# Twelve instead of eight pairs of row tiles by seven products in the second feed-forward product, with weight sums formed by adding transfers

## The chip, the core and the metric

The kernel runs on one core of one Trainium2 chip. The metric is the device time in microseconds of one execution. The engines that matter are TensorE (PE: matmuls, with PEld for its weight loads), VectorE (DVE), ScalarE (ACT), GpSimd (POOL) and SyncE (SP); SP and POOL, and here and there ACT, issue the transfers (DMA) between the chip's memory (HBM) and the on-chip memory (SBUF). Matmul results stand in eight banks of PSUM, 128 partitions x 512 float32 each.

## The reference

One layer of an encoder: 512 tokens, model width 1024. After a mixing part (gated MLP and attention) comes the feed-forward part, whose second product is what changes:

```python
h = h + rms_norm(mix_out, norm_mix_post)
n2 = rms_norm(h, norm_mlp_pre)
hid = jnp.square(jax.nn.relu(n2 @ w_up))       # (512, 4096)
mlp_out = hid @ w_down                         # w_down: (4096, 1024)
h = h + rms_norm(mlp_out, norm_mlp_post)
```

All values are float32. The kernel multiplies in float32r: each operand is split into a high part (rounded) and a low part (the rest), and a product is three matmuls, high x high, high x low, low x high.

## The kernel before

**Stages.** The mixing part, then the first feed-forward product, whose result `hid` stands in SBUF as four tiles of eight row tiles (128 rows of the inner width 4096 each, by 512 tokens), three in the pool `hida` and the last in `hidb`; then the second product, in which `hid` is the stationary operand and `w_down` moves. Its result needs all eight banks: four token tiles of 128 x two column halves of 512. The program names them as quarters: X = tokens 0 to 255, columns 0 to 511; W = the same tokens, columns 512 to 1023; Y and Z the same columns for tokens 256 to 511. Each quarter is two banks.

**Plain row tiles.** `plain(f2)` (L1045) loads 1 MB, two row tiles of `w_down`, on SP (L1048), splits `hid` and the weights, and for each row tile adds into all eight banks: 8 x 3 = 24 matmuls (`acc3`, L1041 to L1043). 16 of the 32 row tiles are done so (`F7 = KF - 2 * N7`, `N7 = 8`).

**Seven products.** The other 16 row tiles form two blocks (`c`) of four pairs. In each block `hid` is cut into a11, a12 (tokens 0 to 255) and a21, a22 (tokens 256 to 511), `w_down` into b11, b12 and b21, b22 (the first index is the half of the pair, the second the column half). Seven products of sums replace eight: (a11 - a21) x (b22 - b12), a11 x b11, s2 x (b11 - b12 + b22) with s2 = a22 - a11 + a21, (a11 + s2) x (b22 - the last sum), (a12 - s2) x b22, a22 x (b21 - the sum), a12 x b21. One product of one block is 24 matmuls, which the code calls a chunk (half of it a piece).

**Sums before.** The sums of weights stand in `tsum` (pool `sumpool`) and in `t1`, and DVE forms them: `b22 - tsum` in `first_sums` (L1098), `tsum + b11` and `b21 - tsum` in `two` (L1091), `b22 - tsum` into `t1` (L1150). The activations' sums are formed in place in `hid` and in `s2` (L1099, L1101, L1124, L1125).

**Splits.** `split_into` (L79, L80) is an ACT copy (high) and a DVE subtraction (low). Weight splits go into the tag `hl` of the pool `wback` (five buffers), activation splits into `hhl` (`d0pool` for the first, then `dpool`, three buffers), raw weights into the tag `raw` (two buffers of 1 MB).

**The eight buffers n2.** The tag `n2` of `n2pool` has eight buffers of 512 KB. In this stage it holds, in program order: `gain`, two `b22` and `s2` for block 0, the same for block 1, `v`, four `t1`, and at the end `h2` and two result tiles `o2`.

**What sets the order.** The program lists work in program order; a planner then simulates it and writes each engine's order, and gives out the buffers. `tc.issue_after(ins)` keeps what stands in it behind `ins` on the engine of `ins`. Each engine and each DMA-issuing queue then works strictly in its written order, waiting on semaphores.

**Order of the quarters before.** Plain row tiles 0 to 9; Y += (a11 - a21) x tsum; X and Y by a11 x b11 and s2 x tsum in turn; `v` = Y + X's sum (L1133); plain row tiles 10 to 15; Z and W in turn; Y and X, the last block one token tile after the other. What a quarter had gathered before a product that others share is copied away (`r22`, `p1`, `r12`, `z0`, in a buffer of `hida`) and put back by DVE sums (L1130 to L1142, L1176 to L1178). `weigh` and `finish` (L1156 to L1172) then do the norm: ACT sums squares, DVE multiplies by `gain`, POOL takes the power (L96), DVE scales and adds `h2` (L1166), SP writes the halves out (L1168). `h2` is read back from memory by POOL (L1158).

Of the kernel before, what the change touches and what calls it, by code (L numbers as in the profile page):

```python
# [16 lines left out]
P = 128  # L17
# [19 lines left out]
def block_kernel(ctx: ExitStack, tc: tile.TileContext, x, norm_mix_pre, w_in, b_gate, ln_v_gain, ln_v_bias,  # L37
# [987 lines left out]
    N7 = 8  # L1025
    F7 = KF - 2 * N7
    FA = 10
# [17 lines left out]
    def plain(f2, order):  # L1045
# [4 lines left out]
        for j in range(2):  # L1050
            wh, wl = split_back(raw[:, j], [D])
            for t, hf in order:
                acc3(accs[t][hf], (hh[:, j, tsl[t]], hl[:, j, tsl[t]]), (wh[:, halves[hf]], wl[:, halves[hf]]),
                     f + j == 0, f + j in (FA - 1, F7 - 1))

    w7 = w_down[F7 * P:].rearrange("(c j h p) d -> c h p j d", p=P, h=2, j=4)

    def block(c, h, hf):
        raw = raw_down()
        raw = raw.rearrange("p a (b d) -> p (a b) d", d=512)  # L1060
        nc.sync.dma_start(raw, w7[c, h, :, :, halves[hf]])
        return raw

# [6 lines left out]
    def chunk(ps, h, w, stop):  # L1070
        for i in range(2):
            piece(ps, h, w, i, stop and i == 1)

    def piece(ps, h, w, i, stop=False):
        (hh, hl), (wh, wl) = h, w[i]
        for j in range(2):
            for t in range(2):
                acc3(ps[t], (hh[:, 2 * i + j, tsl[t]], hl[:, 2 * i + j, tsl[t]]), (wh[:, j], wl[:, j]), False, stop and j == 1)

    order = [(t, hf) for t in range(4) for hf in range(2)]  # L1080
    y_first = [(2, 0), (3, 0), (0, 0), (1, 0), (0, 1), (1, 1), (2, 1), (3, 1)]
    for f2 in range(3):
        plain(f2, order)
    blk = [hid[F7 // 8 + c].rearrange("p (j h) s -> p j h s", h=2) for c in range(2)]
    a11, a12, a21, a22 = [[b[:, :, h, z * 256:z * 256 + 256] for b in blk] for z in range(2) for h in range(2)]
    tsum = sumpool.tile([P, N7, 512], F32, name="tsum")
    tsum = [tsum[:, 4 * c:4 * c + 4] for c in range(2)]
    s2 = []

    def two(out, x, y, op):  # L1090
        nc.vector.tensor_tensor(out, x, y, op=op)  # L1091

    def first_sums(c):
        nc.sync.dma_start(tsum[c], w7[c, 0, :, :, halves[1]])
        for i in range(0, 4, 2):
            b22 = n2pool.tile([P, 2, 512], F32, name="b22", tag="n2")
            nc.sync.dma_start(b22, w7[c, 1, :, i:i + 2, halves[1]])
            nc.vector.tensor_tensor(tsum[c][:, i:i + 2], b22, tsum[c][:, i:i + 2], op=ALU.subtract)  # L1098
        nc.vector.tensor_tensor(a21[c], a11[c], a21[c], op=ALU.subtract)  # L1099
        s2.append(n2pool.tile([P, 4, 256], F32, name="s2", tag="n2"))  # L1100
        nc.vector.tensor_tensor(s2[c], a22[c], a21[c], op=ALU.subtract)  # L1101

    with tc.issue_after(joined.ins):
        first_sums(0)
    plain(3, order)
    with tc.issue_after(joined.ins):
        first_sums(1)
    plain(4, y_first)
    keep = hida.tile([P, 8, S], F32, name="hid")
    p1, r22, r12, z0 = [keep[:, 2 * i:2 * i + 2] for i in range(4)]  # L1110
    for dst, src in ((r22, Y), (p1, X)):
# [7 lines left out]
    for c in range(2):
        b11 = block(c, 0, 0)  # L1120
        h, w = h_split(a11[c]), w_split(b11)
        two(tsum[c], tsum[c], b11, ALU.add)
        h6, w6 = h_split(s2[c]), w_split(tsum[c])
        nc.vector.tensor_tensor(a11[c], a11[c], s2[c], op=ALU.add)  # L1124
        nc.vector.tensor_tensor(s2[c], a12[c], s2[c], op=ALU.subtract)  # L1125
        for i in range(2):
            piece(X, h, w, i, c == 1 and i == 1)
            piece(Y, h6, w6, i, c == 1 and i == 1)
# [6 lines left out]
    z_first = [(2, 1), (3, 1), (0, 1), (1, 1), (0, 0), (1, 0), (2, 0), (3, 0)]  # L1135
    for f2 in range(FA // 2, F7 // 2):
        plain(f2, z_first)
    for i in range(2):
        nc.scalar.activation(z0[:, i], Z[i], AF.Copy)
    nc.vector.tensor_tensor(r22, v, r22, op=ALU.subtract)  # L1140
    nc.vector.tensor_tensor(r12, v, r12, op=ALU.subtract)
# [40 lines left out]
    for c in range(2):  # L1182
# [4 lines left out]
        if c:  # L1187
            break
# [59 lines left out]
```

## Time and profile before

| | |
|---|---|
| median of 3 runs | 796.56 us (795.64 to 796.91) |
| the profiled execution | 795.91 us, span 794.1 us, mean granted TensorE clock 0.998 |
| busy in the span: PE, DVE, ACT, POOL | 782.3, 590.1, 443.3, 56.8 us |
| second product: first and last matmul | about 617 us (beside the first product's last ones, which end about 629 us) and 786 us |
| second product: matmuls | 720, in three lines of 240 |
| moved over the span | 101 MB, 127 GB/s |

A row of a group is: line, engine, operation, the names of what is written and read, shapes, count, then busy time and mean of one in ns, then the idle time before the group and what ended it. A row of a window is: the stretch, its length, busy time with count for each engine, and at the end the granted TensorE clock, the share of time in which the DMA engines were busy, and GB/s. A row in order of time is: start, duration, engine, line, operation, and in brackets how long the engine had been idle and what it waited for. A matmul shows 0.39 us from its start to its end, but the next one starts before it ends.

### The profile page before, as it was taken

The page shows a single profiled execution, that of the slowest core. Times are in us where ns is not written, and L with a number is a line of the kernel's source. Part 1 is how long each engine was busy: PE and PEld are TensorE (multiplying, and loading weights), DVE is VectorE, ACT ScalarE, POOL GpSimd, SP SyncE. Part 2 cuts the span into 40 slices and gives each one's busy share as a digit, 9 for nine tenths or more (in the row PEclk, how much of TensorE's full clock was granted, in tenths as well). Part 3 has the DMA queues.
Part 4 walks back from the last instruction along what each step waited for, and adds up shares of the span by engine and source line. Part 5 has one row for each costly group of instructions (what it writes and reads, how often), then busy time and mean ns, then how long its engine had stood idle before and what let it go on. Part 6 is the DMA issues. An engine that isn't in the chain of part 4 may idle for free.

```text
span 794.1 us, 12232 instructions
## 1 busy us (share of the span) xinstructions
PE 782.3 (99%) x4869; PEld 710.5 (89%) x4869; DVE 590.1 (74%) x953; ACT 443.3 (56%) x731; POOL 56.8 (7%) x85
## 2 busy tenths in 40 slices
PE   9999999999999999999999999999999999999995
PEld 6899999998988889999988899999999888888884
DVE  6784679978663878788656579898888575786687
ACT  6351568878676555454436447567666534553461
POOL 2300100010003400000000200000000000000001
PEclk9999999999999999999999999999999999999999
DMA  9733733262634534344455222343333840144303
GB/s 303 244 107 106 213 106 107 66 174 57 183 107 113 166 80 108 80 118 121 133 186 186 106 80 71 95 153 109 106 108 106 333 146 25 54 141 151 106 1 132
DMA packets 93739, 101.01 MB, mean 127 GB/s; under 512 B 2754, under 2 KB 74466, under 8 KB 93683
## 3 DMA queue, kind: packets, MB, share of 16 engines
q1 hardware_dynamic: 83344, 79.70, 32.3%
q0 software_dynamic: 10336, 20.54, 8.4%
q8 instruction: 38, 0.62, 0.3%
q14 instruction: 19, 0.15, 0.1%
q10 hardware_dynamic: 2, 0.00, 0.0%
HBM read 90.27 MB, written 9.96 MB: 126 GB/s over the span
## 4 chain that ended last, share of the span: by engine, by line
PE 94%; ACT 2%; DMA 1%; DVE 1%; issue 0%; DVEq 0%; ACTq 0%
PE pacc L974 10%; PE pg L343 9%; PE pd L1041 7%; PE pd L1042 7%; PE pd L1043 7%; PE pgacc L343 6%; PE pf L84 5%; PE pf L85 5%; PE pf L86 5%; PE ptp L974 4%; PE pv L84 4%; PE pv L86 4%; PE pv L85 4%; PE pgS L343 3%; PE pd L85 2%; PE pd L84 2%
## 5 line engine op out<-in xcount | busy, mean ns | idle before, releaser
L1042 PE MATMUL pd<-hl,hhl 128*128 128x512 f32 x240 | 93.2, 389 | 0.0
L1041 PE MATMUL pd<-hl,hhl 128*128 128x512 f32 x240 | 92.3, 389 | 0.0
L1043 PE MATMUL pd<-hl,hhl 128*128 128x512 f32 x240 | 91.1, 389 | 0.0
L974 PE MATMUL pacc<-nt,hl 128*128 128x256 f32 x504 | 67.0, 279 | 0.6 <-DVE u L996 0.6
L974 PEld LDWEIGHTS pacc<-nt,hl 128*128 128x128 f32 x504 | 62.4, 188 | 0.8 <-ACT hid L1012 0.8
L1043 PEld LDWEIGHTS pd<-hl,hhl 128*128 128x128 f32 x240 | 45.1, 188 | 9.5
L1042 PEld LDWEIGHTS pd<-hl,hhl 128*128 128x128 f32 x240 | 45.1, 188 | 9.2
L1041 PEld LDWEIGHTS pd<-hl,hhl 128*128 128x128 f32 x240 | 45.0, 188 | 9.2
L79 ACT ACTIVATE hl<-dnw 128x1024 fp32r<-128x1024 f32 x28 | 29.5, 1056 | 30.2 <-PE pd L1043 20.1
L974 PE MATMUL pacc<-n,hl 128*128 128x256 f32 x336 | 45.1, 279 | 0.0
L74 ACT ACTIVATE hi<-s 128x1024 fp32r<-128x1024 f32 x30 | 31.7, 1058 | 23.5 <-DVE s L330 10.1
L84 PE MATMUL pf<-nh,hi 128*128 128x512 f32 x112 | 44.5, 397 | 0.0
L85 PE MATMUL pf<-nl,hi 128*128 128x512 f32 x112 | 43.9, 392 | 0.0
L86 PE MATMUL pf<-nh,lo 128*128 128x512 f32 x112 | 43.9, 392 | 0.0
L75 DVE TENSOR_TENSOR lo<-s,hi 128x1024 fp32r<-128x1024 f32 x30 | 36.6, 1224 | 9.7 <-ACT hi L74 9.6
L79 ACT ACTIVATE hl<-s 128x1024 fp32r<-128x1024 f32 x28 | 29.4, 1058 | 24.5 <-DVE s L958 14.9
L974 PEld LDWEIGHTS pacc<-n,hl 128*128 128x128 f32 x336 | 41.8, 188 | 0.1
L80 DVE TENSOR_TENSOR hl<-dnw,hl 128x1024 fp32r<-128x1024 f32 x28 | 33.9, 1219 | 7.2 <-ACT hl L79 7.2
L80 DVE TENSOR_TENSOR hl<-s,hl 128x1024 fp32r<-128x1024 f32 x28 | 34.2, 1221 | 5.7 <-ACT hl L79 5.7
L85 PE MATMUL pv<-lo,nh 128*128 128x512 f32 x96 | 38.2, 397 | 0.0
L86 PE MATMUL pv<-hi,nl 128*128 128x512 f32 x96 | 37.6, 396 | 0.0
L84 PE MATMUL pv<-hi,nh 128*128 128x512 f32 x96 | 37.4, 397 | 0.0
(386 smaller groups left out, 2216.6 us busy)
## 6 DMA issues: line engine op xcount, KB each, us to landing
upw<-in_w_up_dram SPq DMA_DIRECT2D x16, 1024.0 KB, 5.5
dnw<-in_w_down_dram SPq DMA_DIRECT2D x14, 1024.0 KB, 4.8
qkw<-in_w_in_dram SPq DMA_DIRECT2D x24, 512.0 KB, 5.2
gw<-in_w_in_dram SPq DMA_DIRECT2D x16, 512.0 KB, 5.2
slab<-in_w_in_dram SPq DMA_DIRECT2D x6, 1024.0 KB, 8.9
wow<-in_w_out_dram SPq DMA_DIRECT2D x4, 1024.0 KB, 4.9
w0raw<-in_w_in_dram SPq DMA_DIRECT2D x4, 512.0 KB, 7.2
v0d<-v POOLq DMA_DIRECT2D x4, 512.0 KB, 4.6
```

The source lines that it names most:

```text
L74: nc.scalar.activation(hi, raw, AF.Copy)
L75: (sub or nc.vector).tensor_tensor(lo, raw, hi.bitcast(F32), op=ALU.subtract)
L79: nc.scalar.activation(hi, src, AF.Copy)
L80: return sub.tensor_tensor(lo, src, hi.bitcast(F32), op=ALU.subtract)
L84: nc.tensor.matmul(ps, ah, bh, start=start, stop=False)
L85: nc.tensor.matmul(ps, ah, bl, start=False, stop=False)
L86: return nc.tensor.matmul(ps, al, bh, start=False, stop=stop)
L343: nc.tensor.matmul(ps, a[:, j], b[:, j], start=first and not (j or i), stop=(j == KH - 1 and i == 2), skip_group_check=True)
L974: nc.tensor.matmul(ps, a[:, j], b[:, j], start=first and not (j or m), stop=(j == KH - 1 and m == 2), skip_group_check=True)
L1041: nc.tensor.matmul(ps, ah, bh, start=start, stop=False, skip_group_check=True)
L1042: nc.tensor.matmul(ps, ah, bl, start=False, stop=False, skip_group_check=True)
L1043: return nc.tensor.matmul(ps, al, bh, start=False, stop=stop, skip_group_check=True)
```

## The change

- `N7` goes from 8 to 12: 8 row tiles stay plain, and 24 (three blocks) are done by seven products. All plain row tiles now stand before the products; none is left between them.
- Weight sums are formed by transfers that add into SBUF (`add_block`, issued by POOL, `accum_op=ALU.add`): b22, then b11, then b21 are added into `tsum`; `t1` is loaded with b11 by SP and b12 is added to it by POOL. DVE forms no weight sum any more.
- Since transfers only add, the signs change: tsum is b12 + b22 (+ b11, + b21), s2 is a21 - a11 - a22; the copies are taken off with other signs.
- The order of the quarters: Y, X, Y again, Z, W, Y, X, each with the three blocks in a row, no two quarters in turn. The last block of the last Y and X goes one token tile after the other.
- `z0` is copied with `r22` and `p1`. The n2 tag holds no `b22`, three `s2`, six `t1`, and at the end four result tiles `o` and four `h2`; `finish` asks for `h2` after the power instead of first, and writes the second half out on ACT's queue.

```diff
-    N7 = 8
+    N7 = 12
+    NC = N7 // 4
     F7 = KF - 2 * N7
-    FA = 10
...
+    def add_block(dst, c, h, hf, js=slice(0, 4)):
+        nc.gpsimd.dma_start(dst, w7[c, h, :, js, halves[hf]], accum_op=ALU.add)
...
-    def chunk(ps, h, w, stop):
-        for i in range(2):
-            piece(ps, h, w, i, stop and i == 1)
...
+        for j in range(4):
+            wh, wl = w[j // 2]
+            for t in range(2):
+                acc3(ps[t], (hh[:, j, tsl[t]], hl[:, j, tsl[t]]), (wh[:, j % 2], wl[:, j % 2]), False, stop and j == 3)
+        yield None
+
+    def run(*args):
+        for _ in chunk(*args):
+            pass
...
     def first_sums(c):
         nc.sync.dma_start(tsum[c], w7[c, 0, :, :, halves[1]])
-        for i in range(0, 4, 2):
-            b22 = n2pool.tile([P, 2, 512], F32, name="b22", tag="n2")
-            nc.sync.dma_start(b22, w7[c, 1, :, i:i + 2, halves[1]])
-            nc.vector.tensor_tensor(tsum[c][:, i:i + 2], b22, tsum[c][:, i:i + 2], op=ALU.subtract)
+        add_block(tsum[c], c, 1, 1)
         nc.vector.tensor_tensor(a21[c], a11[c], a21[c], op=ALU.subtract)
         s2.append(n2pool.tile([P, 4, 256], F32, name="s2", tag="n2"))
-        nc.vector.tensor_tensor(s2[c], a22[c], a21[c], op=ALU.subtract)
...
+        nc.vector.scalar_tensor_tensor(s2[c], a21[c], -1.0, a22[c], op0=ALU.mult, op1=ALU.subtract)
+
+    plain(0, order)
+    for f2 in range(1, F7 // 2):
+        plain(f2, order if f2 < F7 // 2 - 1 else y_first)
+        with tc.issue_after(joined.ins):
+            first_sums(f2 - 1)
...
+    for c in range(NC):
+        run(Y, h_split(a21[c]), w_split(tsum[c]), c == NC - 1)
+        add_block(tsum[c], c, 0, 0)
     for i in range(2):
         nc.scalar.activation(r12[:, i], Y[i], AF.Copy)
...
+    for c in range(NC):
+        run(X, h_split(a11[c]), w_split(block(c, 0, 0)), c == NC - 1)
     for i in range(2):
         nc.vector.tensor_tensor(p1[:, i], X[i], p1[:, i], op=ALU.subtract)
+    t1 = []
+    for c in range(NC):
+        run(Y, h_split(s2[c]), w_split(tsum[c]), c == NC - 1)
+        add_block(tsum[c], c, 1, 0)
+        nc.vector.tensor_tensor(a11[c], a11[c], s2[c], op=ALU.add)
+        nc.vector.tensor_tensor(s2[c], a12[c], s2[c], op=ALU.add)
     v = n2pool.tile([P, 2, 512], F32, name="v", tag="n2")
     for i in range(2):
         nc.vector.tensor_tensor(v[:, i], Y[i], p1[:, i], op=ALU.add)
...
+    for c in range(NC):
+        w = []
+        for i in range(2):
+            js = slice(2 * i, 2 * i + 2)
+            t1 = n2pool.tile([P, 2, 512], F32, name="t1", tag="n2")
+            nc.sync.dma_start(t1, w7[c, 0, :, js, halves[0]])
+            add_block(t1, c, 0, 1, js)
+            w.append(split_back(t1, [2, 512]))
+        run(Z, h_split(a11[c]), w, c == NC - 1)
+    nc.vector.tensor_tensor(r22, r22, v, op=ALU.subtract)
+    nc.vector.tensor_tensor(r12, r12, v, op=ALU.subtract)
     nc.vector.tensor_tensor(r12, r12, z0, op=ALU.subtract)
...
+    for c in range(NC):
+        run(W, h_split(s2[c]), w_split(block(c, 1, 1)), c == NC - 1)
...
+    def finish(t, src, y, early, ss):
+        o = n2pool.tile([P, D], F32, name="o", tag="n2")
+        weigh(src, y, o[:, halves[0]], ss, 0)
+        r = rstd_of(ss, 1.0 / D)
+        h2 = n2pool.tile([P, D], F32, name="h2", tag="n2")
+        nc.gpsimd.dma_start(h2, h2d[tsl[t]])
+        for hs, part in zip(halves, (y, early)):
+            nc.vector.scalar_tensor_tensor(o[:, hs], part, r, h2[:, hs], op0=ALU.mult, op1=ALU.add)
+        for hs, eng in zip(halves, (nc.sync, nc.scalar)):
+            eng.dma_start(out[tsl[t], hs], o[:, hs])
...
+    for c in range(NC):
+        for t in chunk(Y, h_split(a22[c]), w_split(tsum[c]), c == NC - 1, c == NC - 1):
+            if t is not None:
                 nc.vector.tensor_tensor(p1[:, t], Y[t], p1[:, t], op=ALU.add)
-                finish(2 + t, [p1[:, t], None], [p1[:, t], r22[:, t]], o, sums[2 + t])
-            else:
-                finish(t, [X[t], None], [None, r12[:, t]], o, sums[t])
+                finish(2 + t, p1[:, t], p1[:, t], r22[:, t], sums[2 + t])
+    for c in range(NC):
+        for t in chunk(X, h_split(a12[c]), w_split(block(c, 1, 0)), c == NC - 1, c == NC - 1):
+            if t is not None:
+                finish(t, X[t], lpool.tile([P, 512], F32, name="y"), r12[:, t], sums[t])
```

More of the change, by code (lines that the diff above doesn't have):

```diff
@@ L1080, in block_kernel @@
+    def run(*args):
+        for _ in chunk(*args):
+            pass
     order = [(t, hf) for t in range(4) for hf in range(2)]
[L1081 to L1084, printed above, removed]
+    y_first = [(2, 0), (3, 0), (0, 0), (1, 0), (2, 1), (3, 1), (0, 1), (1, 1)]
+    blk = [hid[F7 // 8 + c].rearrange("p (j h) s -> p j h s", h=2) for c in range(NC)]
@@ L1117, in block_kernel @@
     for i in range(2):
         nc.scalar.activation(r12[:, i], Y[i], AF.Copy)
[L1119 to L1128, printed above, removed]
+    for c in range(NC):
+        run(X, h_split(a11[c]), w_split(block(c, 0, 0)), c == NC - 1)
@@ L1133, in block_kernel @@
         nc.vector.tensor_tensor(v[:, i], Y[i], p1[:, i], op=ALU.add)
[L1135 to L1141, printed above, removed]
-    nc.vector.tensor_tensor(r12, r12, z0, op=ALU.subtract)
-    for c in range(2):
-        b22 = block(c, 1, 1)
-        h, w = h_split(s2[c]), w_split(b22)
-        h5, w5 = h_split(a11[c]), []
-        for i in range(2):
-            t1 = n2pool.tile([P, 2, 512], F32, name="t1", tag="n2")
-            nc.vector.tensor_tensor(t1, b22[:, 2 * i:2 * i + 2], tsum[c][:, 2 * i:2 * i + 2], op=ALU.subtract)
-            w5.append(split_back(t1, [2, 512]))
-        for i in range(2):
-            piece(Z, h5, w5, i, c == 1 and i == 1)
-            piece(W, h, w, i, c == 1 and i == 1)
-    def finish(t, srcs, ys, o, ss):
-        h2 = n2pool.tile([P, D], F32, name="h2", tag="n2")
-        nc.gpsimd.dma_start(h2, h2d[tsl[t]])
-        for hf in (1, 0):
-            if srcs[hf] is not None:
-                if ys[hf] is None:
-                    ys[hf] = lpool.tile([P, 512], F32, name="y")
-                weigh(srcs[hf], ys[hf], o[:, halves[hf]], ss, hf)
-        r = rstd_of(ss, 1.0 / D)
-        for hf, hs in enumerate(halves):
-            nc.vector.scalar_tensor_tensor(o[:, hs], ys[hf], r, h2[:, hs], op0=ALU.mult, op1=ALU.add)
-        for hs in halves:
-            nc.sync.dma_start(out[tsl[t], hs], o[:, hs])
+    for c in range(NC):
[9 more added lines that the diff above has]
+    nc.vector.tensor_tensor(r12, r12, v, op=ALU.subtract)
+    nc.vector.tensor_tensor(r12, r12, z0, op=ALU.subtract)
+    for c in range(NC):
+        run(W, h_split(s2[c]), w_split(block(c, 1, 1)), c == NC - 1)
     def weigh(src, y, junk, ss, hf):
@@ L1174, in block_kernel @@
     sums = [small.tile([P, 2], F32, name="ss2") for _ in range(4)]
     for i in range(2):
+        nc.vector.tensor_tensor(r22[:, i], Z[i], r22[:, i], op=ALU.add)
+        weigh(r22[:, i], r22[:, i], v[:, i], sums[2 + i], 1)
+        nc.vector.tensor_tensor(r12[:, i], Z[i], r12[:, i], op=ALU.add)
         nc.vector.tensor_tensor(r12[:, i], W[i], r12[:, i], op=ALU.add)
-        nc.vector.tensor_tensor(r12[:, i], Z[i], r12[:, i], op=ALU.add)
-        nc.vector.tensor_tensor(r22[:, i], Z[i], r22[:, i], op=ALU.add)
```

52 lines of the change are left out of this document (13 added, 39 removed).

## The prediction

> **What bounds the kernel now.** I read the page first (busy shares, chain of waits, groups), then the windows over the second product, then the waits and the order in time of the engines around the edit.
>
> ```profile
> span 794.1 us, 12232 instructions
> PE 782.3 (99%) x4869; PEld 710.5 (89%) x4869; DVE 590.1 (74%) x953; ACT 443.3 (56%) x731; POOL 56.8 (7%) x85
> PE 94%; ACT 2%; DMA 1%; DVE 1%; issue 0%; DVEq 0%; ACTq 0%
> L1042 PE MATMUL pd<-hl,hhl 128*128 128x512 f32 x240 | 93.2, 389 | 0.0
> L1041 PE MATMUL pd<-hl,hhl 128*128 128x512 f32 x240 | 92.3, 389 | 0.0
> L1043 PE MATMUL pd<-hl,hhl 128*128 128x512 f32 x240 | 91.1, 389 | 0.0
> ```
>
> TensorE sets the end: 94% of the chain, and the second product's 720 matmuls (three lines of 240) have no idle time before them. The next rows are the windows over that stage, all engines, and then the tile pd (the product's banks) alone over 100 us.
>
> ```profile
> 685.00:705.00 20.00, 20.00 (x90) 16.57 (x89) 16.08 (x15) 11.37 (x12) 0.00 (x0) 1.00 0.26 97
> 705.00:725.00 20.00, 20.00 (x90) 16.58 (x89) 16.28 (x16) 8.16 (x8) 0.54 (x1) 1.00 0.47 162
> ...
> 650.00:750.00 100.00, 100.00 (x443) 82.84 (x442) 2.65 (x4) 4.53 (x8) 1.00 0.27 92
> ```
>
> 443 matmuls touch 100 us and each shows 0.39 us, so one starts every (100+0.39)/443 = **0.2266 us**. That, not the 389 ns, is the price of one. VectorE (DVE) reaches 16.3 of 20 us and the DMA share 0.47: neither ends a wait of TensorE here, but both have to keep ahead of it.
>
> **Matmuls removed.** A row tile of W_down costs 4 token tiles x 2 column halves x 3 = 24 matmuls in the plain form; a pair of row tiles costs 7 products x 2 token tiles x 3 = 42 by seven products, against 48. Before: 16 x 24 + 8 x 42 = 720. After: 8 x 24 + 12 x 42 = 696. The gain is 24 x 0.2266 = **-5.4 us**, all of it on the path.
>
> **Sums and splits.** The additions that go and those that stay on DVE have these groups; the last two rows are one split of weights into high and low parts.
>
> ```profile
> L1098 DVE TENSOR_TENSOR tsum<-b,tsum 128x1024 f32<-128x1024 f32 x4 | 4.8, 1215 | 0.0
> L1150 DVE TENSOR_TENSOR t<-dnw,tsum 128x1024 f32<-128x1024 f32 x4 | 4.7, 1223 | 1.9 <-DMA dnw<-in_w_down_dram 1.9
> L1091 DVE TENSOR_TENSOR tsum<-dnw,tsum 128x2048 f32<-128x2048 f32 x2 | 4.6, 2294 | 0.4 <-DMA dnw<-in_w_down_dram 0.3
> L1091 DVE TENSOR_TENSOR tsum<-tsum,dnw 128x2048 f32<-128x2048 f32 x2 | 4.6, 2292 | 0.1
> L80 DVE TENSOR_TENSOR hl<-t,hl 128x1024 fp32r<-128x1024 f32 x4 | 4.9, 1222 | 1.5 <-ACT hl L79 1.5
> L79 ACT ACTIVATE hl<-t 128x1024 fp32r<-128x1024 f32 x4 | 4.2, 1051 | 4.5 <-issue 3.5 <-PE pd L1043 1.0
> ```
>
> DVE loses 4.8+4.7+4.6+4.6 = 18.7 us of sums. It gains 9 more splits (66 become 75: 44+22 of weights and activations before, 50+25 after; 11.0 us) and the four activation sums of a third block (4.9 us). The net is -2.8 us under a TensorE that covers it: **0**. Without cover the 9 splits would cost 9 x 1.22 us.
>
> **Transfers added.** Loads of 1 MB go from 18 (8 plain, 10 for two blocks) to 19 plain loads and 12 MB of adding transfers, all on POOL's queue (per block: b22, b11 and b21 into tsum, b12 into the two halves of t1). Next come, in order, the landing times of the 1 MB loads (tile dnw), of the 512 KB loads on POOL (tile h), of the 512 KB loads in a crowd (tile b), and the window of that crowd.
>
> ```profile
> DMA to landing us min/median/max: 4.7/4.9/7.3
> DMA to landing us min/median/max: 3.4/4.1/4.5
> DMA to landing us min/median/max: 3.4/8.2/8.9
> 625.00:630.00 5.00, 5.00 (x31) 4.42 (x31) 2.02 (x4) 1.44 (x2) 0.00 (x0) 1.00 1.05 394
> ```
>
> 512 KB more cost 4.7 - 3.4 = 1.3 us in an empty queue, 2.1 us being fixed. No row shows an adding transfer. From below it costs what a plain load costs, 3.4 us (it moves at least those bytes, which excludes a gain); from above I take the crowded 8.9 us. Logically it reads its destination as well, twice the reading, so I take the median plus one more reading: 4.1+1.3 = **5.4 us** for 512 KB, 2.6 us of it queue time. On average that fits: 19 x 2.6 + 12 x 5.2 = 112 us in a stage of 696 x 0.2266 = 158 us. The question is where one is waited for. The Trainium skill (Collectives: The Full Stack, "The bandwidth ceiling") has an add in the transfer running at half a copy's rate, because of its two reads; by that page the sum stays what I have, and nothing here shows it.
>
> **Where it is waited for.** Call 0 the end of the third run of seven (Y += s2 x tsum), after which the new order puts (a11) x (b11+b12) on Z. Before, plain row tiles lay between v and Z's products; now nothing does. t1 lives in the eight buffers n2, behind v. How the planner gives these buffers out is seen in POOL's order and one row of ScalarE (ACT):
>
> ```profile
> 723.39 0.54 POOL L1158 DMA_DIRECT2D h<-h2d  x1 [106.92 <-DVE hhl L80]
> 737.82 0.53 POOL L1158 DMA_DIRECT2D h<-h2d  x1 [13.89 <-DVE hl L80]
> 739.75 0.53 POOL L1158 DMA_DIRECT2D h<-h2d  x1 [1.41 <-DVE hl L80]
> ...
> 783.70 0.57 POOL L1158 DMA_DIRECT2D h<-h2d  x1
> ...
> 783.33 0.60 ACT L1171 ACTIVATE o<-pd 128x512 f32<-128x512 f32 x1 [1.27 <-PE pd L1043]
> ```
>
> h2's source is long written, and between the last sum of L1098 and v only gain and the two s2 hold one of the eight buffers; yet h2's first load comes after v and all four t1 (L1150) have theirs, when an s2 is split; the fourth waits until the result tile written before it in the program (783.33) has begun. So I read: buffers of one tag are given in program order, and an engine's order follows that. In the new kernel the planner then can place t1's load only after v; in its order of time v's two sums and the three sums behind them (r22, r12 twice) come before t1's split, and each engine keeps that order. Their rows:
>
> ```profile
> 711.43 0.68 DVE L1133 TENSOR_TENSOR v<-pd,hid 128x512 f32<-128x512 f32 x1
> ...
> 714.30 1.21 DVE L1140 TENSOR_TENSOR hid<-v,hid 128x1024 f32<-128x1024 f32 x1
> 715.44 1.21 DVE L1141 TENSOR_TENSOR hid<-v,hid 128x1024 f32<-128x1024 f32 x1
> ```
>
> The second v cannot start before Y's last matmul, at about 0.05, and takes 0.6 to the next; three sums at a pitch of 1.14 take 3.4; the low part of t1 then runs 4.1 to 5.3. Z's first piece starts at **5.3**, where it would have started at 0. Queued behind that wait on DVE is the whole chain of Z's splits.
>
> Is t1 itself in time? Splits run five weight buffers ahead, each waiting for TensorE to release one:
>
> ```profile
> ACT hl L79 <- PE pd L1043: 32.5, 16, 5.7
> ```
>
> A piece of 12 matmuls is 2.72 us and a run of six pieces 16.3. The last split of tsum starts when the first piece of its run is done, -16.3+2.7 = -13.6, and ends at about -11.1; POOL then issues tsum's last 1 MB add (4.9+2.6 = 7.5, landed at -3.6), and t1's three queued halves land at about -1.0, 1.6 and 4.2. DVE's order hides that much.
>
> What is late next: only three n2 buffers are left for t1's six halves (gain, three s2 and v hold five). The fourth half waits for the first split to release its buffer (5.3), then load 4.1, add 5.4, split 1.05+1.22: ready at 17.1. TensorE has worked off three pieces at 5.3+8.2 = 13.5 and waits **3.6 us**. From below, load 3.4 and add 3.4: 14.4, a wait of 0.9; from above, add 8.9: 20.6, 7.1. The other two halves follow within a piece. Together 5.3+3.6 = **+8.9** (6.2 to 12.4).
>
> The other waits on adds have room: the first tsum sums are needed some 43 us after their loads (8 x 24 matmuls of plain tiles), the later ones 16 us and more.
>
> **The clock.** The granted clock falls after TensorE stops:
>
> ```profile
> 780.00:795.00 15.00, 6.01 (x27) 4.66 (x25) 8.93 (x17) 2.56 (x8) 3.63 (x5) 0.86 0.49 175
> ```
>
> If it falls to half, 0.14 of the 14.1 us recorded there is 3.9 us at half rate before 794.1, so it fell some 4 us after the last matmul at 786.0. A gap of 5.3 us can reach that, and the next pieces would run slowly; but they end in the wait for the fourth half, so this adds nothing unless that wait is short. The Trainium skill (TensorE: Matmul & The Clock Gate, Part 1) gives half rate after an idle window of about 3.4 us and the same again to release it; the row agrees in kind, and by the page the sum would change by an estimated 1.7 us only where the second wait is gone.
>
> **The tail.** The last rows before:
>
> ```profile
> 785.63 0.39 PE L1043 MATMUL pd<-hl,hhl 128*128 128x512 f32 x1
> 786.05 0.60 ACT L1171 ACTIVATE o<-pd 128x512 f32<-128x512 f32 x1 [2.03 <-PE pd L1043]
> 786.50 0.15 DVE L93 SCALAR_TENSOR_TENSOR rs_in<-ss,rs_in 128x1 f32<-128x1 f32 x1
> 786.55 0.19 ACT L1171 ACTIVATION_READ_ACCUMULATOR o<-pd 128x1 f32 x1
> 786.81 0.56 POOL L96 TENSOR_TENSOR rs_out<-rs_in,neghalf 128x1 f32<-128x1 f32 x1 [2.54 <-DVE rs_in L93]
> ...
> 789.43 0.74 DVE L1166 SCALAR_TENSOR_TENSOR o<-hid,rs_out,h 128x512 f32<-128x512 f32 x1
> ```
>
> The last scaled sum ends 4.15 us after the last matmul, behind seven other long DVE operations. Now two token tiles finish 16 us earlier and take their part out, but h2 of the last tile is issued behind the previous tile's power on POOL: that tile stops 2.7 us before the end, 0.8 ACT, 0.15 DVE, 0.56 POOL, so issue at -1.2, landing (3.4 to 4.5) at 2.2 to 3.3, two sums 1.4: end at 3.6 to 4.7. **0**, between -0.5 and +0.5. The second output on ACT's queue is within that.
>
> **Sum.** 795.91 (profiled execution, span 794.1 and 1.8 around it) - 5.4 + 8.9 + 0 = 799.4; against the median of 796.56 it would be 800.1. I say **799.5**, with 796.5 to 803 as its own range (waits of 6.2 to 12.4).
>
> **Rivals.** (1) The planner places t1's loads and adds ahead of v, and DVE's order has the split first. For it: its three buffers are free then, and all sources are in memory; against: the four h2 rows. Both waits shrink to under 2 us: 795.9 - 5.4 + 0 to 2 = **790.5 to 792.5**, faster. Decided by t1's first low part ending before v.
> (2) One of the two waits alone: 795.9 - 5.4 + 5.3 = **795.8**, or with 3.6 alone 794.1. For it: the two come from different causes; against: the buffer count makes the second follow from the first.
> (3) Adds set the pace: once 512 KB need more than a piece's 2.72 us of queue time (I have 2.6), Z runs at their rate. At 4 us: tsum's add lands at -0.8, the sixth half at 23.2, split and piece 5.0, an end at 28 instead of 16.3: +12, **802 to 805**. For it: my value is just below the point; against: the crowded window moved 394 GB/s, so the engines have room.
> (4) The change doesn't act: if the longer tsum (24 KB for 16 KB in a partition) had to wait for the first product's buffers, its sums would start some 10 us later; 43 us of plain tiles cover it, so no time of its own.
>
> **How the numbers follow.** Forecast 0.48; (1) 0.30; (2) 0.11; (3) 0.11. A measurement here tells 0.2%, 1.6 us, from no change. Faster: (1) and a little of (2), 0.33. Same: the rest of (2) and the forecast's low edge, 0.14. Slower: 0.53. The range reaches from (1) to the nearer part of (3): 790.0 to 804.5.
>
> **What would show it.** 696 matmuls at 0.2266; a gap of about 5 us before Z's first piece whose releaser is DVE's low part of t, with the sums of v, r22 and r12 straight before it; a second gap three pieces later behind an add on t; h2's last load behind a power. If TensorE has no gap above 1 us in the stage, (1) was right; if the gaps end with adding transfers that queue on one another, (3).

## The result and the profile after

The changed kernel takes 803.97 us (median of 4 runs, 803.54 to 804.27) against 796.10 us of the kernel before in the same comparison (795.63 to 796.91): ratio 1.0097, 95% interval 1.008 to 1.0115, slower by 7.9 us where 3.4 were forecast. Later, beside other experiments, the same changed kernel took 802.56 us (801.99 to 804.37) against 796.89, slower by 5.7 us, ratio 1.0077 (1.0065 to 1.009). The profiled execution took 804.06 us. First the page of its profile: span, busy shares, and the second product's groups with the idle time before them.

```profile
span 802.3 us, 12254 instructions
PE 781.8 (97%) x4845; PEld 708.1 (88%) x4845; DVE 587.2 (73%) x954; ACT 452.3 (56%) x740; POOL 75.8 (9%) x100
L1042 PE MATMUL pd<-hl,hhl 128*128 128x512 f32 x232 | 91.8, 396 | 3.1 <-DVE hl L80 3.1
L1041 PE MATMUL pd<-hl,hhl 128*128 128x512 f32 x232 | 90.3, 397 | 4.6 <-ACT hl L79 4.6
```

The 696 matmuls are there (three lines of 232; the third is L1043), 24 fewer than before, but two of the lines now have idle time, 7.7 us together. The order in time of TensorE, cut to the matmuls beside each stop, shows where (start, duration, engine, line, operation, tiles, count, idle time before it and what ended it):

```profile
715.95 0.39 PE L1043 MATMUL pd<-hl,hhl 128*128 128x512 f32 x1
719.27 1.09 PE L1041 MATMUL pd<-hl,hhl 128*128 128x512 f32 x2 [2.93 <-ACT hl L79]
722.93 0.80 PE L1042 MATMUL pd<-hl,hhl 128*128 128x512 f32 x1 [2.57 <-DVE hl L80]
...
732.12 0.39 PE L1043 MATMUL pd<-hl,hhl 128*128 128x512 f32 x1
734.18 0.74 PE L1041 MATMUL pd<-hl,hhl 128*128 128x512 f32 x2 [1.68 <-ACT hl L79]
735.44 0.50 PE L1042 MATMUL pd<-hl,hhl 128*128 128x512 f32 x1 [0.52 <-DVE hl L80]
...
793.63 0.39 PE L1043 MATMUL pd<-hl,hhl 128*128 128x512 f32 x1
```

The matmul at 715.95 is the last of Y's third run, so 0 of the prediction's clock is 715.95 + 0.23 = 716.18. There are exactly two stops in the whole second product: ahead of Z's first piece and three pieces later. Between 715.95 and 793.63 lie 288 matmuls, 65.3 us at 0.2266; they took 77.7, so **12.4 us** are lost there, where the prediction had 8.9. VectorE's order around the first stop:

```profile
715.70 1.37 DVE L1135 TENSOR_TENSOR v<-pd,hid 128x512 f32<-128x512 f32 x2 [2.44 <-PE pd L1043]
717.10 1.22 DVE L1146 TENSOR_TENSOR hid<-hid,v 128x1024 f32<-128x1024 f32 x1
718.25 1.22 DVE L1147 TENSOR_TENSOR hid<-hid,v 128x1024 f32<-128x1024 f32 x1
719.38 1.22 DVE L80 TENSOR_TENSOR hhl<-hid,hhl 128x1024 fp32r<-128x1024 f32 x1
720.52 1.22 DVE L1148 TENSOR_TENSOR hid<-hid 128x1024 f32<-128x1024 f32 x1
721.65 2.35 DVE L80 TENSOR_TENSOR hl<-t,hl 128x1024 fp32r<-128x1024 f32 x2
```

This is the predicted list (v twice, the three sums on r22 and r12, then t's low part), with one item more: at 719.38 the low part of a block of activations. The next three fences are GpSimd's adds into t1, ScalarE's first splits of t1's halves, which start as soon as the adds have landed, and SyncE's loads of the last three halves, the fourth first.

```profile
706.44 1.29 POOL L1064 DMA_DIRECT2D tsum<-in_w_down_dram  x1 [4.42 <-DVE hl L80]
707.18 4.21 POOL L1064 DMA_DIRECT2D t<-in_w_down_dram  x3
726.83 1.20 POOL L1064 DMA_DIRECT2D t<-in_w_down_dram  x1 [15.44 <-DMA t<-in_w_down_dram]
```

```profile
718.16 1.06 ACT L79 ACTIVATE hl<-t 128x1024 fp32r<-128x1024 f32 x1 [0.73 <-DMA t<-in_w_down_dram]
720.70 1.06 ACT L79 ACTIVATE hl<-t 128x1024 fp32r<-128x1024 f32 x1 [1.48 <-DMA t<-in_w_down_dram]
723.24 1.06 ACT L79 ACTIVATE hl<-t 128x1024 fp32r<-128x1024 f32 x1 [1.48 <-DMA t<-in_w_down_dram]
...
733.07 1.06 ACT L79 ACTIVATE hl<-t 128x1024 fp32r<-128x1024 f32 x1 [2.19 <-DMA t<-in_w_down_dram]
```

```profile
722.90 3.06 SPq L1142 DMA_DIRECT2D t<-in_w_down_dram  x3
```

The three queued halves land one every 2.54 us. The fourth is asked for only when the first has been split (about 722.8), its add is issued at 726.83 and has landed at 733.07.

### The profile page after: what moved, and what is told of

The parts are those of the page before. It is cut to its first block, busy times and chain, and to the rows that moved or that the text cites. A ratio compares the mean times of both kernels' runs of the same rounds, so it can differ in the third digit from the quotient of the medians.

```text
span 802.3 us, 12254 instructions
## 1 busy us (share of the span) xinstructions
PE 781.8 (97%) x4845; PEld 708.1 (88%) x4845; DVE 587.2 (73%) x954; ACT 452.3 (56%) x740; POOL 75.8 (9%) x100
## 3 DMA queue, kind: packets, MB, share of 16 engines
q0 software_dynamic: 16720, 33.12, 17.1%
## 4 chain that ended last, share of the span: by engine, by line
PE 91%; DMA 3%; ACT 2%; DVE 2%; issue 1%; POOLq 0%; DVEq 0%; POOL 0%
PE pacc L974 10%; PE pg L343 9%; PE pd L1042 6%; PE pd L1041 6%; PE pd L1043 6%; PE pgacc L343 6%; PE pf L84 5%; PE pf L85 5%; PE pf L86 5%; PE ptp L974 4%; PE pv L84 4%; PE pv L86 4%; PE pv L85 4%; PE pgS L343 3%; PE pd L85 2%; PE pd L84 2%
## 5 line engine op out<-in xcount | busy, mean ns | idle before, releaser
L1042 PE MATMUL pd<-hl,hhl 128*128 128x512 f32 x232 | 91.8, 396 | 3.1 <-DVE hl L80 3.1
L1041 PE MATMUL pd<-hl,hhl 128*128 128x512 f32 x232 | 90.3, 397 | 4.6 <-ACT hl L79 4.6
L1043 PE MATMUL pd<-hl,hhl 128*128 128x512 f32 x232 | 90.2, 394 | 0.0
L1041 PEld LDWEIGHTS pd<-hl,hhl 128*128 128x128 f32 x232 | 44.1, 191 | 14.5 <-ACT hl L79 5.5
L1042 PEld LDWEIGHTS pd<-hl,hhl 128*128 128x128 f32 x232 | 44.4, 192 | 13.4 <-DVE hl L80 4.2
L1043 PEld LDWEIGHTS pd<-hl,hhl 128*128 128x128 f32 x232 | 44.3, 191 | 9.4
L80 DVE TENSOR_TENSOR hhl<-hid,hhl 128x1024 fp32r<-128x1024 f32 x19 | 23.1, 1222 | 20.2 <-ACT hhl L79 20.2
L79 ACT ACTIVATE hl<-dnw 128x1024 fp32r<-128x1024 f32 x26 | 27.0, 1053 | 17.9 <-PE pacc L974 8.3
## 6 DMA issues: line engine op xcount, KB each, us to landing
slab<-in_w_in_dram SPq DMA_DIRECT2D x6, 1024.0 KB, 10.1
```

Of the source, the lines that this page charges most:

```text
L79: nc.scalar.activation(hi, src, AF.Copy)
L80: return sub.tensor_tensor(lo, src, hi.bitcast(F32), op=ALU.subtract)
L1041: nc.tensor.matmul(ps, ah, bh, start=start, stop=False, skip_group_check=True)
L1042: nc.tensor.matmul(ps, ah, bl, start=False, stop=False, skip_group_check=True)
L1043: return nc.tensor.matmul(ps, al, bh, start=False, stop=stop, skip_group_check=True)
```

## The experiments

One number makes the profiles comparable: where the last matmul starts. Before, that is 785.63; 24 matmuls less would make it 785.63 - 5.44 = 780.19. "Lost" is how much later than 780.19 a kernel's last matmul starts in its profiled run, one of the runs in the range beside it. Each ratio is to the kernel before in the same set of runs (medians of before: 796.1 to 796.9).

| kernel | time us (range) | ratio, 95% interval | lost us |
|---|---|---|---|
| changed | 803.97 (803.54 to 804.27) | 1.0097, 1.0080 to 1.0115 | 13.4 |
| changed, again | 802.56 (801.99 to 804.37) | 1.0077, 1.0065 to 1.0090 | 11.9 |
| three sums later | 802.95 (802.31 to 804.71) | 1.0085, 1.0070 to 1.0100 | 12.8 |
| v in other tiles | 793.94 (793.68 to 794.26) | 0.9970, 0.9958 to 0.9982 | 2.9 |
| plain instead of adding transfers | 801.09 (800.14 to 802.48) | 1.0060, 1.0043 to 1.0077 | 10.4 |
| two blocks | 805.78 (805.23 to 806.27) | 1.0117, 1.0102 to 1.0132 | 9.7 (from 785.63) |
| adds on VectorE | 804.24 (803.75 to 805.08) | 1.0095, 1.0082 to 1.0109 | 13.1 |
| v moved, adds on VectorE, rows first | 798.47 (796.87 to 800.05) | 1.0022, 1.0013 to 1.0031 | 10.6 |
| zero matmuls in the stops, twice | 803.91 (802.05 to 805.74); 805.06 (802.90 to 805.17) | 1.0090, 1.0073 to 1.0107; 1.0096, 1.0083 to 1.0110 | 12.5; 12.3 |
| third block in a raw buffer | 806.73 (806.39 to 808.44) | 1.0128, 1.0114 to 1.0142 | 17.3 |
| rows first | 803.37 (801.48 to 804.30) | 1.0081, 1.0067 to 1.0094 | 13.8 |
| t1 asked for ahead of v | 797.46 (796.18 to 798.17) | 1.0007, 0.9997 to 1.0017 | 5.0 |
| v moved, rows first | 792.80 (792.42 to 793.29) | 0.9951, 0.9935 to 0.9967 | 2.6 |
| v moved, third block raw, rows first | 791.04 (790.95 to 791.35) | 0.9930, 0.9916 to 0.9943 | 0.9 |

**The changed kernel once more**, unedited, beside three of the kernels below:

> The changed kernel once more, beside the next three on one chip, so that differences of 1 us can be read: 803.5 to 804.5 by every theory.

802.56 us, 1 us below that, with runs between 801.99 and 804.37. Differences of less than 2 us between kernels that have the stops are not read from medians below.

**The order on VectorE alone.** The three sums go behind the last split of t1 (the list `lows` collects the splits):

```diff
-    nc.vector.tensor_tensor(r22, r22, v, op=ALU.subtract)
-    nc.vector.tensor_tensor(r12, r12, v, op=ALU.subtract)
-    nc.vector.tensor_tensor(r12, r12, z0, op=ALU.subtract)
+    with tc.issue_after(lows[-1].ins):
+        nc.vector.tensor_tensor(r22, r22, v, op=ALU.subtract)
+        nc.vector.tensor_tensor(r12, r12, v, op=ALU.subtract)
+        nc.vector.tensor_tensor(r12, r12, z0, op=ALU.subtract)
```

> The three sums on r22 and r12 after v are put on VectorE behind the last low part of t1 that is split before Z's first matmuls; nothing else is changed, all work stays. Theory (the order on VectorE is what the first wait of the Z product is made of, 6.7 us in the changed kernel): the first wait ends on ScalarE's high part and then on VectorE's low part about 2.2 to 2.4 us earlier, at some 4.4 us, the buffer of v does not come free earlier (its last reader is moved back), so the second wait stays at 3 us or grows by up to 2.4; the time goes to between 801.5 and 804. Rival (the adding DMAs' own landing sets the first wait): the first wait stays over 6 us and the time stays at 804.

802.95 us, no difference from the changed kernel. TensorE's two stops in it (Y's last matmul starts at 715.06 here; line numbers in this kernel are one higher, so its L1042 and L1043 are L1041 and L1042 above):

```profile
719.68 0.80 PE L1043 MATMUL pd<-hl,hhl 128*128 128x512 f32 x1 [0.18 <-DVE hl L80]
732.74 1.22 PE L1042 MATMUL pd<-hl,hhl 128*128 128x512 f32 x2 [3.96 <-ACT hl L79]
```

The low part is there 719.68 - 715.29 = 4.4 us after Y's end instead of 6.75, as the theory said. What sets these 4.4 us is the landing of t1's first half, for which ScalarE waits until 717.32, 2.0 us after Y's end; in the changed kernel it lands as late, and then stands behind VectorE's list:

```profile
717.32 1.06 ACT L79 ACTIVATE hl<-t 128x1024 fp32r<-128x1024 f32 x1 [0.77 <-DMA t<-in_w_down_dram]
```

The second stop grows from 1.7 to 4.0 us and takes the gain back: up to the second low part 10.1 us are lost instead of 10.6, and the slow matmuls behind it (see "The clock" below) cost 2.5 instead of 1.8. The buffer of the first half comes free 2.3 us sooner, but then the fourth half's load and add need 12.0 us (719.66 to 731.63 in the order of time) instead of 10.3. Why they take longer is open. The DMA engines are full in the window from 728 to 732 us, first row (length, clock, DMA share, GB/s), but they are so in the changed kernel too, second row:

```profile
728.00:732.00 4.00, 1.00 1.13 214
```

```profile
728.00:732.00 4.00, 1.00 1.04 253
```

So VectorE's list sets the last 2.35 us of the first stop, and the end of Z hangs on the fourth half.

**The price of adding.**

```diff
-        nc.gpsimd.dma_start(dst, w7[c, h, :, js, halves[hf]], accum_op=ALU.add)
+        nc.gpsimd.dma_start(dst, w7[c, h, :, js, halves[hf]])
```

> All adding transfers on GpSimd's queue become plain transfers of the same blocks to the same places in the same order: the sums of weight blocks are left out (the output is that of other weights), all other work is the same. Theory (order, not the price of adding): the first wait keeps about 5 to 6.7 us, since VectorE's own list before the first low part is as long, and the second shrinks by 1.5 to 2.5 us: 800 to 802.5. Rival (the price of adding, 2.5 us for 512 KB against 1.3 plain, is the loss): both waits nearly vanish, 791 to 794.

801.09 us, inside the theory's range. The issues of the transfers in the changed kernel (count, KB each, median us from issue to landing), and then in this one:

```profile
tsum<-in_w_down_dram POOLq DMA_DIRECT2D x9, 1024.0 KB, 8.6
t<-in_w_down_dram POOLq DMA_DIRECT2D x6, 512.0 KB, 9.1
```

```profile
tsum<-in_w_down_dram POOLq DMA_DIRECT2D x9, 1024.0 KB, 5.7
t<-in_w_down_dram POOLq DMA_DIRECT2D x6, 512.0 KB, 5.7
```

A megabyte takes 2.9 us more when it is added, about the 2.6 that the prediction put on a second reading. The first stop nonetheless stays (the low part comes 6.7 us after Y's end: 722.57 - 715.83), with all three halves landed when ScalarE gets to them; the second shrinks to 0.6 us. Adding costs 1.5 to 2.9 us (against 802.56 and 803.97; the smaller of the two is within the spread of these kernels). The chain to the fourth half is shorter: its low part is used 733.97 - 715.83 = 18.1 us after Y's end instead of 19.2.

**Adds on VectorE instead.**

```diff
-        nc.gpsimd.dma_start(dst, w7[c, h, :, js, halves[hf]], accum_op=ALU.add)
+        raw = raw_down().rearrange("p a (b d) -> p (a b) d", d=512)[:, js]
+        nc.sync.dma_start(raw, w7[c, h, :, js, halves[hf]])
+        nc.vector.tensor_tensor(dst, dst, raw, op=ALU.add)
```

> The changed kernel, each adding transfer replaced by a plain load into a raw buffer on the sync engine's queue and an addition on VectorE (2.3 us for a block, 1.1 us for a half); order and buffers of v and t1 stay. Theory (what Z waits for first is VectorE's list between Y and the first low part): the list gets two additions longer, the first wait grows from 6.7 to 9 to 11 us, the time goes up to 806 to 812. Rival (adding in the transfer is the loss, 2.5 us a half instead of 1.3): without it 795 to 800.

> As the kernel with v in other tiles (793.9), with additions on VectorE in place of the adding transfers, and the loads of the last residual rows asked for before the powers. Theory (once the order is mended the adding transfers are the cheaper way, because VectorE has the splits to do and the raw buffers are two): 795 to 802. Rival (adding transfers cost more than VectorE's additions even so): 791 to 793.

With v where the change has it: 804.24 us. The list got longer as foreseen, and the first low part came 724.37 - 715.35 = 9.0 us after Y's end, but the second stop became shorter (2.0 us, with no slow matmuls behind it), so the total missed both forecasts. With v moved (next experiment) and the rows first (see "The tail" below), the additions on VectorE gave 798.47 us against 792.80 with adding transfers: adding in the transfer is the cheaper way, and not what made most of the loss.

**v out of the buffers of t1.** v goes to two tiles of a pool that is idle then; the sums with v are done in halves.

```diff
-    v = n2pool.tile([P, 2, 512], F32, name="v", tag="n2")
+    v = [lpool.tile([P, 512], F32, name="v", tag="y") for _ in range(2)]
```

> v is written into two tiles of another pool of its own time instead of an n2 buffer, so that t1 has four free buffers and its first loads and adds can be issued before the last sums. Theory (the price is in the order: buffers and the queue of VectorE's and GpSimd's programs, not in the adding DMAs as such): no wait in Z's product, no slow-clock stretch there, 12.5 us of loss gone: between 790.5 and 793. Rival (three adding blocks are too much for the DMA queue whatever their order): the waits move to the Y products whose sums are then later, and the time stays over 799.

793.94 us, 8.6 to 10.0 us less than the changed kernel and 0.3% less than before, though 0.9 us above the theory's range. GpSimd's order in it, and VectorE's:

```profile
644.75 1.16 POOL L1064 DMA_DIRECT2D t<-in_w_down_dram  x1 [7.71 <-DMA t<-in_w_down_dram]
...
664.97 1.17 POOL L1064 DMA_DIRECT2D t<-in_w_down_dram  x1 [9.55 <-PE pd L1043]
...
717.44 1.17 POOL L1064 DMA_DIRECT2D t<-in_w_down_dram  x1 [5.39 <-DVE hl L80]
723.45 1.20 POOL L1064 DMA_DIRECT2D t<-in_w_down_dram  x1 [4.83 <-DMA t<-in_w_down_dram]
```

```profile
716.05 1.23 DVE L80 TENSOR_TENSOR hl<-t,hl 128x1024 fp32r<-128x1024 f32 x1
717.19 1.29 DVE L1135 TENSOR_TENSOR v<-pd,hid 128x512 f32<-128x512 f32 x2
```

Four adds into t1 now run between 644 and 666 us, ahead of the last tsum sums, and four low parts are done before v. Only the last two halves still wait for a buffer (717.44, 723.45), and TensorE loses 2.3 us to them.

**Order or number of buffers?** v stays in an n2 buffer, but t1's first four halves are asked for ahead of it:

```diff
+    ws = [t1_split(c) for c in range(NC - 1)]
     v = n2pool.tile([P, 2, 512], F32, name="v", tag="n2")
...
-        run(Z, h_split(a11[c]), w, c == NC - 1)
+        run(Z, h_split(a11[c]), ws[c] if c < NC - 1 else t1_split(c), c == NC - 1)
```

> The changed kernel, v still in an n2 buffer, but the first four halves of t1 are asked for ahead of v in the program instead of behind it; t1 then has the four buffers first and v gets the first one that t1 frees. Number of buffers, transfers and work are the same. Theory (order in the program): the first wait and the second are gone, the last two halves of t1 are one buffer later than in the kernel with v moved, whose waits there were 2.3 us: 793 to 798. Rival (number of buffers): v or t1 waits instead, 800 to 804.

797.46 us: 5 to 6.5 us less than the changed kernel, from the order of two statements. The first stop is gone; one is left, ahead of the third block:

```profile
728.39 0.73 PE L1041 MATMUL pd<-hl,hhl 128*128 128x512 f32 x2 [2.39 <-ACT hl L79]
```

So the program's order, by which buffers are handed out and engines' lists are laid, is over half of what moving v brings. The rest, 797.46 against 793.94, goes with the fourth buffer that t1 then has; this is the difference of the two kernels, and no run shows it alone.

**Only t1's third block elsewhere, v in place.** The block goes whole into a raw weight buffer:

```diff
+        if c == NC - 1:
+            t1 = block(c, 0, 1)
+            add_block(t1, c, 0, 0)
+            w = w_split(t1)
```

> The changed kernel with v left in its n2 buffer, and only the third block of t1 loaded whole into a raw weight buffer. Theory (v ahead of t1 is what holds the fourth half and the order): the first wait stays at 6.3 us or more, the second at 2 to 4 us, since the fourth half still waits for a buffer: 803 to 805. Rival (too few buffers for t1 as a whole, whoever holds them): one transfer chain less, both waits shrink, 793 to 798.

806.73 us, worse than either forecast. GpSimd now has ten 1 MB adds ahead of t1's instead of nine, and the first stop is the longest of all:

```profile
724.99 1.22 PE L1041 MATMUL pd<-hl,hhl 128*128 128x512 f32 x2 [8.11 <-ACT hl L79]
```

t1's first add is issued 8.5 us ahead of Y's end (9.0 in the changed kernel), but it has landed only 7.4 us behind it instead of 2.0. That is 5.4 us more; one more megabyte of adds, at two queue times of 2.54 us, would account for it, which is argued and not shown. So the run moves the queue of adds along with the buffer and does not test the buffer alone; relief in buffers did not help while the order stayed.

**Two blocks in the new structure.**

```diff
-    N7 = 12
+    N7 = 8
```

> Two of the four quarters go by seven products, in the changed kernel's structure with adding transfers (N7 = 8, 720 matmuls of the second product instead of 696): 24 matmuls come back (+5.4 us), and v and the four halves of t1 have a buffer each. Theory (buffers): the first wait of Z's product stays, 5 to 7 us, the second is gone with its 3.1 us and its slow-clock stretch of 1.6 us: 804.0 + 5.4 - 4.7 = 804.7, between 802.5 and 806.5. Rival (the number of adding transfers in the queue makes both waits): both gone, 804.0 + 5.4 - 12.5 = 796.9, 796 to 798.

805.78 us, with the 24 matmuls back. The first stop is there (the low part used at 749.63, 6.75 us after Y's end at 742.88, as in the changed kernel), the second is not, as the theory said. The slow matmuls behind the stop have no second wait to be hidden in here: of the 9.2 us lost from Y's end on, 6.3 are the stop and 2.9 these matmuls. Two blocks in this structure lose 9.7 us of TensorE's time to the kernel before, which does the same two blocks.

**The clock.** Matmuls that add zeros to Z fill the stops (26 ahead of Z, 12 ahead of the second half of its second block).

```diff
+            nc.tensor.matmul(Z[0], zero[:, :P], zero, start=False, stop=False, skip_group_check=True)
```

> The changed kernel with 38 more matmuls that add zeros to the Z sums: 26 ahead of Z's first matmul (26 x 0.227 = 5.9 us, inside the first wait of 6.7) and 12 ahead of the last half of its second block (2.7 us, inside the second wait). Nothing that Z waits for is moved. Theory (the halved clock after the waits is a cost of its own, the part behind the second wait is not hidden): the granted clock stays near 1 through 716 to 740 us, the matmuls behind the second wait are 0.23 us apart instead of 0.43, the second wait gets longer by what the first stretch gains, and the time falls by 1.4 to 1.8 us to between 802.0 and 802.8. Rival (the clock is hidden by the waits, as the prediction had it): 803.5 to 804.3, no change.

> The kernel with 38 zero matmuls in the two waits once more, now beside the changed kernel. Theory (halved clock behind the second wait is a cost of its own): 1.0 to 1.8 us less than the changed kernel in the same runs. Rival (hidden, or given back by matmuls that are in the way): within 0.5 us of it.

803.91 and 805.06 us: no gain, and in the second set 2.5 us more than the changed kernel, which I cannot explain from the profiled run (802.90). Windows over TensorE (from:to, length, busy, granted clock, DMA share, GB/s) in the changed kernel, in its other profiled execution, and with zero matmuls (second set):

```profile
722.00:729.00 7.00, 6.07 (x20) 0.69 0.63 197
734.00:741.00 7.00, 6.29 (x19) 0.76 0.74 172
```

```profile
722.00:729.00 7.00, 6.38 (x18) 0.62 0.66 213
734.00:741.00 7.00, 6.28 (x26) 1.00 0.78 181
```

```profile
722.00:729.00 7.00, 6.76 (x30) 1.00 0.77 235
734.00:741.00 7.00, 6.04 (x25) 1.00 0.72 162
```

Zero matmuls keep the clock at 1.00 throughout, and the second half of Z's second block still starts where it did (low part used at 735.70 against 735.44 and 735.46), since its weights come no sooner. The slow matmuls behind the first stop cost nothing, as the prediction said. Those behind the second cost 1.8 us in one execution of the changed kernel and 0.2 in the other. The Trainium skill (TensorE: Matmul & The Clock Gate, Part 1) has the window run free of what the kernel does, so that its phase decides; two executions with nearly the same stops and a different clock agree. The clock record of the traces shows the phase: the full-rate stretch ahead of the first slow one lasts 706.56 us in the one and 709.97 in the other, the slow stretches 6.83 and 3.41 in the one and 6.83 in the other, which are 207, 208, 2, 1 and 2 times 3.413 us.

**The tail.** h2's load stands ahead of the power, in `finish`:

```diff
+        h2 = n2pool.tile([P, D], F32, name="h2", tag="n2")
+        nc.gpsimd.dma_start(h2, h2d[tsl[t]])
         o = n2pool.tile([P, D], F32, name="o", tag="n2")
         weigh(src, y, o[:, halves[0]], ss, 0)
         r = rstd_of(ss, 1.0 / D)
-        h2 = n2pool.tile([P, D], F32, name="h2", tag="n2")
-        nc.gpsimd.dma_start(h2, h2d[tsl[t]])
```

> The changed kernel, only the load of the residual rows of each last tile asked for before the power of its norm. The kernel that had this edit beside others ended 3.8 us after its last matmul, the changed kernel 5.0 us. Theory (order on GpSimd and VectorE in the tail, on the path): 1.0 to 1.3 us less than the changed kernel. Rival (the tail's end is set by the last matmul alone): no change.

> The kernel with v moved (793.94 in its runs), and only the loads of the residual rows asked for before the powers. Theory (the tail's 1.2 us are on the path): 1.0 to 1.4 us less, 792.5 to 793.0, with 2.3 us of waits left in Z that the third block in a raw buffer took away. Rival (no gain): 793.5 to 794.3.

VectorE's last rows in the changed kernel, whose last matmul ends at 794.02, and then with this edit, where it ends at 794.41:

```profile
794.78 0.69 DVE L1154 TENSOR_TENSOR y<-pd,gain 128x512 f32<-128x512 f32 x1 [1.96 <-ACT o L1153]
795.39 0.74 DVE L1163 SCALAR_TENSOR_TENSOR o<-y,rs_out,h 128x512 f32<-128x512 f32 x1
...
798.29 0.75 DVE L1163 SCALAR_TENSOR_TENSOR o<-hid,rs_out,h 128x512 f32<-128x512 f32 x1
```

```profile
793.96 0.75 DVE L1163 SCALAR_TENSOR_TENSOR o<-y,rs_out,h 128x512 f32<-128x512 f32 x1 [0.75 <-POOL rs_out L96]
...
797.43 0.75 DVE L1163 SCALAR_TENSOR_TENSOR o<-hid,rs_out,h 128x512 f32<-128x512 f32 x1
```

In the changed kernel the last tile's product stands ahead of the previous tile's two sums, and VectorE idles 1.96 us for it; with the edit the sums come first, and the last one ends 3.8 instead of 5.0 us after the last matmul. In the changed kernel that 1.2 us drowned in the spread of Z's stops (803.37 against 802.56, ranges overlapping; up to the last matmul the profiled run lost 1.9 us more, 13.8 against 11.9). With v moved, where the times spread less, it shows: 792.80 against 793.94.

**A version that is faster than both.** v in other tiles, the third block of t1 in a raw buffer, the rows first:

> v in two tiles of its own, the third block of t1 loaded whole into a raw weight buffer (free from the end of X's second product on) instead of two n2 halves, and the loads of the last residual rows asked for before the powers. Theory (order and buffers are all of the loss): the last 2.3 us of waits in Z that the kernel with v moved alone has left go too, 24 matmuls of 0.2266 fewer are all that is left of the change: 796.3 - 5.4 = 790.9, with the tail between 790.3 and 791.7. Rival (the adding transfers in the queue delay something else once they are earlier): 793 to 796.

791.04 us, ratio to before 0.993 (0.9916 to 0.9943). All engines in the 20 us around Z's start (busy and count of PE, PEld, DVE, ACT, POOL, then clock, DMA share, GB/s):

```profile
715.00:735.00 20.00, 20.00 (x90) 16.57 (x89) 18.36 (x20) 10.17 (x10) 1.09 (x2) 1.00 0.83 240
```

No stop is left, at full clock, with VectorE at 18.4 of 20 us. Its span of 789.0 us is 5.1 below that of the kernel before: 5.4 of the matmuls and 0.6 of the tail, less 0.9 that the last matmul comes late. These 0.9 arise ahead of the second product's last 288 matmuls; their cause is open.

## Why the prediction was right and wrong

The profiled execution stands at 802.3 - 794.1 = +8.2 us of span. By the prediction's terms:

| term | predicted | measured |
|---|---|---|
| 24 matmuls | -5.4 | -5.4 |
| ahead of Z | 0 | +1.0 (0.7 in the second execution) |
| first wait, to Z's first low part | +5.3 | +6.3 |
| slow matmuls behind it | 0 | +1.7 (2.3), taken out of the next wait |
| second wait | +3.6 | +2.6 (2.4) |
| slow matmuls behind that | 0 | +1.8 (0.2) |
| tail, to the span's end | 0 | +0.2 |
| sum | +3.5 | +8.2 |

**Right:** the direction; that buffers of one tag are handed out in program order, so that t1 comes behind v; VectorE's list; two stops at the two places; the fourth half waiting for the first one's buffer; the queue time of an add (2.6 estimated, 2.54 measured); 696 matmuls at the old pace. Asking for v behind t1 took the first stop away, and moving v out of n2 nearly all of both, which shows the cause by experiment. Rival (1), t1 placed ahead of v, was the right picture of the kernel that the change could have been: 790.5 to 792.5 there, 791.04 with both repairs and the tail.

The sum came out 4.7 us too low: 1.7 in the two waits, 1.8 in the clock, 1.0 ahead of Z, 0.2 at the end.

**Wrong: the sum "5.3+3.6 = +8.9".** Up to the second low part it measured 6.3 + 1.7 + 2.6 = 10.6 us (11.0 in the second execution). Two of its sizes were short. VectorE's list before t1's first low part left out a split of activations (719.38, 1.14 us), so that the first buffer came free 722.8 - 716.2 = 6.6 us after Y's end, not 5.3. And the fourth half's add took 726.83 to 733.07 = 6.2 us, not 5.4. Both lie on one chain: ready at 735.4 - 716.2 = 19.2 instead of 17.1 us. "5.3" and "3.6" were never two causes that add up; the chain to the fourth half sets the end, and the first wait only divides it. The experiment with the three sums later showed it: 2.35 us off the first wait, 0.5 off the way to the second low part, nothing off the total.

**Wrong, but hidden: "t1's three queued halves land at about -1.0, 1.6 and 4.2".** They landed at 2.0, 4.5 and 7.1 (718.16, 720.70 and 723.24, less 716.18). tsum's last add, ahead of them in the queue, was issued at -9.7 instead of -11.1, and the DMA engines were full ahead of it (share 1.10 from 695 to 716 us, against 0.75 with plain transfers). VectorE's list was longer still, so this cost nothing in the changed kernel; without the list it is what leaves a first wait of 4.4 us.

**Wrong: "this adds nothing" for the clock.** The argument held for the first stop. It overlooked that the second stop has a slow stretch of its own with no wait behind it to hide in: 1.8 us in the profiled execution, 0.2 in the other. It is there in full in one of these two executions, so it is counted as part of the spread rather than as a fixed price of the change.

**Not in the sum:** 1.0 us ahead of Z. In the profiled execution 0.9 of it stands at a wait in the first product, whose code the change leaves alone; the waits of TensorE give it 0.6 before (first row) and 1.5 after (second), and 0.7 in the changed kernel's second execution:

```profile
PE pacc L974 <- DVE u L996: 0.6, 1, 0.6
```

```profile
PE pacc L974 <- DVE u L996: 1.5, 1, 1.5
```

In the second execution this wait is back within 0.1 us of the kernel before, yet 0.7 us are missing ahead of Z. The profiled runs that change nothing in this part of the program show 0.1 (three sums later) to 1.3 (third block in a raw buffer). So the cause of this term is open; as far as these few executions go, it varies from one to the next and is not put down to the change.

**The tail** was within its bounds at the span's end (+0.2), but its last sum came at 5.0, past the 4.7 given: the load behind the power was priced right, and what it did to VectorE's order, the last tile's product placed ahead of the previous tile's sums, was not followed.

Rival (3), adds that set the pace, gave a time near the measured one for a wrong reason: plain transfers in their place bring back 1.5 to 2.9 us, and the first stop stays. Its queue does count once the list on VectorE is out of the way, or once another megabyte stands in it. Rival (2), one wait alone, is out. What remains open besides is the spread of the kernels with stops (up to 3.7 us between runs, against 0.4 us of the version without).

## What to carry over

Read a change of the data's path first for what it does to the order in which buffers of one tag are asked for: a tile that is written late, asked for ahead of tiles that could be loaded early, pushes their loads, their adds and their splits behind itself on every queue. When two waits hang on one chain (buffer, load, add, split), price the chain to its end and not the waits; shortening the first only moves time into the second. Take the engine's list before a wait item by item from the loop that runs ahead too, not only from the statements beside the edit.

## What was not expected of the hardware

An adding transfer holds GpSimd longer: 1.27 us an issue of 1 MB against 0.75 for the same plain transfer, and 1.2 against 0.7 for 512 KB. A 512 KB add with none ahead of it took 6.2 us to land (726.83 to 733.07); a queue of them passed one every 2.54 us, and a megabyte landed in 8.6 us against 5.7. The Trainium skill (Collectives: The Full Stack, "The bandwidth ceiling") names, for the add of a ReduceScatter, its two source reads as what halves the rate; for the adding load here, the 2.9 us between these two medians, beside 2.6 for the plain megabyte's queue time, agree.

At the first stop the clock fell to half 3.3 us after Y's end in the profiled execution and 4.6 us after it in the other; it was back 3.4 and 4.7 us after the first low part let TensorE go on. At the second stop, 1.83 + 0.81 us of lost time with two matmuls between them were followed by slow matmuls, though each pause is shorter than the 3.3 us after which the first stop slowed down; 1.57 + 0.81 in the other execution were not. Whether the two pauses count together, or the moment at which they fall decides, is not shown.
